# Loads of two tiles by one DMA in a strided mean-removal kernel

## The chip, the cores and the metric

One Trainium2 chip, one core of it. The metric is the device time of one execution in microseconds (us), lower is better. The profile's span is about 1.8 us shorter than that of its own run.

## The reference

```python
def reference(x):                       # x: (8, 4096, 2112) float32, 277 MB
    B, S, D = x.shape
    stride = 4
    x_r = x.reshape(B, S // stride, stride, D)
    pooled = x_r.mean(axis=2)
    upsampled = np.repeat(pooled, stride, axis=1)
    return (x - upsampled).astype(np.float32)
```

From each group of four rows its mean is taken off. 276.8 MB have to be read and as many written.

## The kernel before

A tile is 128 groups: 128 partitions x 8448 floats (33,792 bytes a partition, contiguous in HBM). There are 64 tiles and six slots in SBUF. SyncE issues the loads, VectorE (DVE) sums and subtracts in place, ScalarE's queue issues the stores.

```python
    slots = [io_pool.tile([P, W], f32, name=f"slot{b}") for b in range(SLOTS)]   # SLOTS = 6
    ...
    laps, rest = divmod(n, SLOTS)                                                # n = 64
    with tc.tile_critical():
        for k in range(n):
            b, lap = k % SLOTS, k // SLOTS
            load = nc.sync.dma_start(out=slots[b][:], in_=xg[k * P:(k + 1) * P])
            if lap:
                load._wait_ge(store_sems[b], 16 * lap)
            load.then_inc(load_sems[b], 16)
        # VectorE, each tile: three tensor_add into s, then slot = -s/4 + slot;
        # the first add waits for load_sems[b]
        ...
        for k in range(n):
            b = k % SLOTS
            store = nc.scalar.dma_start(out=og[k * P:(k + 1) * P], in_=slots[b][:])
            store._wait_ge(done_sem, k + 1)
            store.then_inc(store_sems[b], 16)
```

Of the kernel before, what the change touches and what calls it, by code (L numbers as in the profile page):

```python
# [1 line left out]

# [4 lines left out]

STRIDE = 4
SLOTS = 6  # L10
PAD = 224


@with_exitstack
def kernel(
    ctx: ExitStack,
    tc: tile.TileContext,
    x: bass.AP,
    out: bass.AP,
):  # L20






    nc = tc.nc
    B, S, D = x.shape
    P = nc.NUM_PARTITIONS
    W = STRIDE * D  # L30
    G = (B * S) // STRIDE
    assert S % STRIDE == 0 and G % P == 0
    n = G // P

    xg = x.rearrange("b (g f) d -> (b g) (f d)", f=STRIDE)
    og = out.rearrange("b (g f) d -> (b g) (f d)", f=STRIDE)
    f32 = mybir.dt.float32

    pad_pool = ctx.enter_context(tc.tile_pool(name="pad", bufs=1))
    io_pool = ctx.enter_context(tc.tile_pool(name="io", bufs=1))  # L40
    sum_pool = ctx.enter_context(tc.tile_pool(name="sum", bufs=1))
    psum_pool = ctx.enter_context(
        tc.tile_pool(name="psum", bufs=1, space=bass.MemoryType.PSUM)
    )
    pad_pool.tile([P, PAD], f32, name="pad")
    slots = [io_pool.tile([P, W], f32, name=f"slot{b}") for b in range(SLOTS)]
    s_sb = sum_pool.tile([P, D], f32, name="s_sb")
    s_ps = psum_pool.tile([P, D], f32, name="s_ps")

    load_sems = [tc.alloc_semaphore(f"load{b}") for b in range(SLOTS)]  # L50
    store_sems = [tc.alloc_semaphore(f"store{b}") for b in range(SLOTS)]
    step_sem = tc.alloc_semaphore("step")
    done_sem = tc.alloc_semaphore("done")

    adds = STRIDE - 1

    def reduce_tile(b, landed):
        rows = slots[b].rearrange("p (f d) -> p f d", f=STRIDE)
        s = s_ps if b % 2 else s_sb
        done = b * adds  # L60
        for f in range(1, STRIDE):
            first = rows[:, 0, :] if f == 1 else s[:]
            add = nc.vector.tensor_add(out=s[:], in0=first, in1=rows[:, f, :])  # L63
            if f == 1:
                add._wait_ge(load_sems[b], landed)
            else:
                add._wait_ge(step_sem, done + f - 1)
            add.then_inc(step_sem)
        sub = nc.vector.scalar_tensor_tensor(  # L69
            out=rows,  # L70
            in0=s[:, None, :].to_broadcast([P, STRIDE, D]),
            scalar=-1.0 / STRIDE,
            in1=rows,
            op0=mybir.AluOpType.mult,
            op1=mybir.AluOpType.add,
        )
        sub._wait_ge(step_sem, done + adds)
        sub.then_inc(done_sem)

    assert SLOTS % 2 == 0  # L80
    laps, rest = divmod(n, SLOTS)
    with tc.tile_critical():  # L82
        for k in range(n):
            b, lap = k % SLOTS, k // SLOTS
            load = nc.sync.dma_start(out=slots[b][:], in_=xg[k * P:(k + 1) * P])
            if lap:
                load._wait_ge(store_sems[b], 16 * lap)
            load.then_inc(load_sems[b], 16)

        with nc.vector.Fori(0, laps) as lap:  # L90
            landed = nc.vector.to_reg(16 * lap + 16)
            for b in range(SLOTS):
                reduce_tile(b, landed)
            nc.vector.wait_ge(step_sem, SLOTS * adds).then_inc(step_sem, -SLOTS * adds)
        for b in range(rest):
            reduce_tile(b, 16 * (laps + 1))

        for k in range(n):
            b = k % SLOTS
# [5 lines that stand above are left out]
    for k in range(n - SLOTS, n):  # L105
        total = nc.gpsimd.to_reg(16 * (k // SLOTS + 1))
        tc.keep_in_program_order(nc.gpsimd.wait_ge(store_sems[k % SLOTS], total))


# [1 line left out]
_INS = ['x']  # L111
_OUTS = [((8, 4096, 2112), 'float32')]


# [23 lines left out]
```

## Time and profile before

| | before |
|---|---|
| time, median of 6 runs | 1284.84 us (1284.71 to 1285.01) |
| profile's span | 1283.3 us |
| VectorE busy | 1026.5 us, 80% |
| the two DMA queues' packets | 100.1% of 16 engines' span |
| bandwidth, windows in the middle | 433 GB/s (435 in two of the 120 us windows) |
| a tile's period | 19.97 us; VectorE needs 16.1 of it |

How to read it: two queues, one of loads and one of stores, are served by the same 16 DMA engines (their packets fill 50.1% and 50.0% of the engines' span). If the engines always have a packet from one queue or the other, the time is the bytes over 433 GB/s and a few us at the ends: the windows quoted in the prediction show 433 with loads alone (4 to 29 us), with stores alone (1270 to 1280) and with both. VectorE's 20% of idle time and the wait before each tile (3.8 us) are a consequence. The number that decides about the change is not on the page: it is how long a load or store waits in its queue behind others, which is called the queues' spare below. The prediction works it out from the page's times from issue to landing.

### The profile page before, as it was taken

What the parts mean: (1) busy time and instruction counts of PE and PEld (TensorE: products, weight loads), DVE (VectorE), ACT (ScalarE), POOL (GpSimd) and SP (SyncE); (2) the same over time, 40 slices, a digit from 0 to 9 for tenths busy, and PEclk for the clock granted to TensorE, in tenths of its full rate; (3) what the DMA queues carried; (4) which work ended last, traced back from release to release, by engine and by line L of the source; (5) the groups of instructions that cost most, each with busy time, mean ns of one, the idle gap of its engine ahead of it and who ended that gap; (6) DMA issues with size and microseconds to landing.
All of it is one profiled execution on the core that took longest, in us unless ns stands there. A gap on an engine that the chain in (4) does not pass through costs nothing.

```text
span 1283.3 us, 483 instructions
## 1 busy us (share of the span) xinstructions
DVE 1026.5 (80%) x256; POOL 0.2 (0%) x4
## 2 busy tenths in 40 slices
DVE  5998788787887877878778787787877878878785
POOL 0000000000000000000000000000000000000000
DMA  9999999999999999999999999999999999999999
GB/s 404 420 436 429 434 437 434 427 437 436 427 436 437 434 427 437 436 427 436 437 433 428 437 436 426 437 437 433 428 437 434 428 437 437 432 429 437 434 427 404
DMA packets 18432, 553.66 MB, mean 431 GB/s; under 512 B 2048, under 2 KB 2048, under 8 KB 2048
## 3 DMA queue, kind: packets, MB, share of 16 engines
q1 hardware_dynamic: 9216, 276.83, 50.1%
q10 hardware_dynamic: 9216, 276.83, 50.0%
HBM read 276.82 MB, written 276.82 MB: 431 GB/s over the span
## 4 chain that ended last, share of the span: by engine, by line
DVE 73%; another core or an unknown queue 24%; DMA 1%; issue 1%; DVEq 0%; SPq 0%
DVE slot L69 38%; DVE s_ps L63 18%; DVE s_sb L63 18%; DMA slot<-in_x_dram 1%; DVEq L90 0%; SPq L133 0%; SPq L82 0%
## 5 line engine op out<-in xcount | busy, mean ns | idle before, releaser
L69 DVE SCALAR_TENSOR_TENSOR slot<-s_sb,slot 128x8448 f32<-128x8448 f32 x32 | 286.7, 8958 | 1.1
L69 DVE SCALAR_TENSOR_TENSOR slot<-s_ps,slot 128x8448 f32<-128x8448 f32 x32 | 286.6, 8957 | 1.1
L63 DVE TENSOR_TENSOR s_sb<-slot 128x2112 f32<-128x2112 f32 x32 | 75.5, 2358 | 123.7 <-DMA slot<-in_x_dram 123.7
L63 DVE TENSOR_TENSOR s_ps<-slot 128x2112 f32<-128x2112 f32 x32 | 75.7, 2367 | 112.1 <-DMA slot<-in_x_dram 112.1
L63 DVE TENSOR_TENSOR s_ps<-s_ps,slot 128x2112 f32<-128x2112 f32 x64 | 151.4, 2366 | 2.2
L63 DVE TENSOR_TENSOR s_sb<-s_sb,slot 128x2112 f32<-128x2112 f32 x64 | 150.9, 2358 | 2.2
L122 POOL MEMSET const-bfloat16-1.0<- 128x1 bf16 x1 | 0.1, 102 | 0.0
L122 POOL MEMSET const-uint8-127<- 128x1 uint8 x1 | 0.1, 102 | 0.0
L122 POOL MEMSET const-float32-0.0<- 128x1 f32 x1 | 0.1, 99 | 0.2 <-issue 0.2
L122 POOL MEMSET const-float32-1.0<- 128x1 f32 x1 | 0.1, 99 | 0.0
## 6 DMA issues: line engine op xcount, KB each, us to landing
slot<-in_x_dram SPq DMA_DIRECT2D x64, 4224.0 KB, 60.1
out_dram<-slot ACTq DMA_DIRECT2D x64, 4224.0 KB, 43.5
```

Of the source, the lines that this page charges most:

```text
L63: add = nc.vector.tensor_add(out=s[:], in0=first, in1=rows[:, f, :])
L69: sub = nc.vector.scalar_tensor_tensor(out=rows, in0=s[:, None, :].to_broadcast([P, STRIDE, D]), scalar=-1.0 / STRIDE, in1=rows, op0=mybir ...
L122: nc = _bacc.Bacc("TRN2", target_bir_lowering=False, num_devices=1)
```

## The change

Intent: fewer, larger load DMAs. In laps 1 to 9 of the ring one DMA fills two neighbouring slots, with two runs of 33,792 bytes a partition, after both slots' stores have landed. One semaphore stands for both tiles: VectorE waits on it for the first one, and the wait left for the second has long been met. The first six tiles and the last four stay single.

```diff
-    slots = [io_pool.tile([P, W], f32, name=f"slot{b}") for b in range(SLOTS)]
+    ring = io_pool.tile([P, SLOTS * W], f32, name="ring")
+    slots = [ring[:, b * W:(b + 1) * W] for b in range(SLOTS)]
...
-        for k in range(n):
+        k = 0
+        while k < n:
             b, lap = k % SLOTS, k // SLOTS
-            load = nc.sync.dma_start(out=slots[b][:], in_=xg[k * P:(k + 1) * P])
+            size = 2 if 0 < lap < laps else 1
+            if size == 2:
+                nc.sync.wait_ge(store_sems[b], 16 * lap)
+            load = nc.sync.dma_start(
+                out=ring[:, b * W:(b + size) * W].rearrange("p (j w) -> p j w", j=size),
+                in_=xg[k * P:(k + size) * P].rearrange("(j p) w -> p j w", j=size),
+            )
             if lap:
-                load._wait_ge(store_sems[b], 16 * lap)
+                load._wait_ge(store_sems[b + size - 1], 16 * lap)
             load.then_inc(load_sems[b], 16)
+            k += size
...
-                reduce_tile(b, landed)
+                reduce_tile(b, 16 if b % 2 else landed)
...
-            reduce_tile(b, 16 * (laps + 1))
+            reduce_tile(b, 32 if b % 2 else 16 * (laps + 1))
```

## The prediction

> **What bounds the kernel now.** I read the page's busy shares and slices first, then its DMA part and groups, then windows at the start, middle and end, then the timeline of the last tiles.

> The page:

> ```profile
> DVE 1026.5 (80%) x256; POOL 0.2 (0%) x4
> ...
> DMA  9999999999999999999999999999999999999999
> ...
> DMA packets 18432, 553.66 MB, mean 431 GB/s; under 512 B 2048, under 2 KB 2048, under 8 KB 2048
> ...
> q1 hardware_dynamic: 9216, 276.83, 50.1%
> q10 hardware_dynamic: 9216, 276.83, 50.0%
> ...
> slot<-in_x_dram SPq DMA_DIRECT2D x64, 4224.0 KB, 60.1
> out_dram<-slot ACTq DMA_DIRECT2D x64, 4224.0 KB, 43.5
> ```

> VectorE (DVE) is 80% busy, the 16 DMA engines 90% or more in every slice, and the two queues' packets fill 100.1% of 16 engines' span. Apart from 2048 small packets (128 DMAs x 16, the completions), every packet is one 33,792-byte row. The last two lines give each DMA's time from issue to landing; I use them as loop times below.

> The windows (start:end, length, DVE busy, POOL busy, clock, DMA share, GB/s):

> ```profile
> 0.00:4.00 4.00, 0.00 (x0) 0.20 (x4) 1.00 0.66 220
> 4.00:13.00 9.00, 0.00 (x0) 0.00 (x0) 1.00 1.03 443
> 13.00:29.00 16.00, 15.57 (x4) 0.00 (x0) 1.00 0.99 427
> 29.00:35.00 6.00, 5.93 (x4) 0.00 (x0) 1.00 1.03 372
> 35.00:51.00 16.00, 15.90 (x5) 0.00 (x0) 1.00 0.98 425
> ...
> 360.00:480.00 120.00, 96.48 (x25) 0.00 (x0) 1.00 1.00 433
> ...
> 1270.00:1275.00 5.00, 0.00 (x0) 0.00 (x0) 1.00 1.00 433
> 1275.00:1280.00 5.00, 0.00 (x0) 0.00 (x0) 1.00 1.00 433
> 1280.00:1283.30 3.30, 0.00 (x0) 0.00 (x0) 1.00 0.36 154
> ```

> Until 29 us there are only loads: (9 x 443 + 16 x 427) / 25 = 433 GB/s. From 1270 there are only stores: 433. In the middle both: 433. So one queue alone is as fast as two together, and only an interval in which **both** queues are empty costs time. The account of the span: 553.65 MB / 433 = 1278 us, 2.0 us before the first byte (220 GB/s x 4 us is 2.0 us' worth of 433), 2.1 us after the last one, about 1.1 us lost at 29 to 51 us as the first stores start; sum 1283.3, as the page says. The measured time is 1.5 us above that span.

> The timeline of the last tiles (start, length, idle before in brackets):

> ```profile
> 1192.79 2.36 DVE L63 TENSOR_TENSOR s_sb<-slot 128x2112 f32<-128x2112 f32 x1 [3.81 <-DMA slot<-in_x_dram]
> ...
> 1252.69 2.37 DVE L63 TENSOR_TENSOR s_ps<-slot 128x2112 f32<-128x2112 f32 x1 [3.84 <-DMA slot<-in_x_dram]
> 1255.09 4.77 DVE L63 TENSOR_TENSOR s_ps<-s_ps,slot 128x2112 f32<-128x2112 f32 x2
> 1259.89 8.96 DVE L69 SCALAR_TENSOR_TENSOR slot<-s_ps,slot 128x8448 f32<-128x8448 f32 x1
> ```

> Three tiles take 59.90 us, 19.97 each; VectorE needs 16.1 of them and waits 3.8 for a load. VectorE is not the bound. (The chain of waits names VectorE for 73% of the span because it follows semaphores; the wait of 3.8 us before each tile says that the load set the pace.)

> [...]

> **The change part by part.**

> Removed: 27 of 64 load DMAs, with 27 x 16 = 432 completion packets, and no byte of data. [...] SyncE's issue time (0.33 us a DMA) is not on the path.

> Added: a wait in SyncE for the first slot's store. That store ends before the second one's, in the same queue, so it costs nothing beyond the wait for the second.

> Moved: a pair is issued when both its stores have landed, and its first tile can't start before both have landed. The latencies from the trace: a load alone lands 12.4 us after issue and moves for 10.0, so 2.4 of latency; a store alone 13.5, so 3.5. The six slots make a loop, whose length is six tiles, 119.8 us. Before: load 20.0 + 2.4, VectorE 16.1, store 20.0 + 3.5, sum 62.0; the other 57.8 us are waiting in the queues: 60.1 - 22.4 = 37.7 behind other loads, 43.5 - 23.5 = 20.0 behind other stores (sum 57.7, which checks). After, for the second tile of a pair: load 39.9 + 2.4, VectorE 32.1, store 20.0 + 3.5, sum 97.9; 21.9 us of waiting remain. Of these 3.9 are the second store behind the first (20.0 less the 16.1 between their issues). So **18.0 us of spare remain, where there were 57.8**. Still positive: the load queue should never be empty until the last load.

> Where the spare lies follows from the passage from singles to pairs. Before, tile 6 started at 114.7. After, it needs its partner too: about 134.7. VectorE ends tile 5 at 110.9, so it idles 24 us instead of 4, and issues store 6 at 150.7. Stores move one per 20 us from 30.5 on, so store 5 leaves the queue at about 150.5: the store queue is empty for about 1 us (issue to first byte, as at the start: 0.95 to 2.0). Load (8,9), allowed by store 3 at about 113, is in its queue by then and takes the bandwidth. Loss: none. From here stores have next to no spare and loads nearly all 18 us.

> The tail, counted from the landing of pair (58,59) as zero: loads 60 to 63 land at 20, 40, 60, 80, all allowed long before. VectorE runs back to back and ends 58 to 63 at 16, 32, 48, 64, 80.3, 96.4. Stores at half speed: 58 from 17 to 37, 59 to 57, 60 to 77, 61 until the loads end at 78.6 and then alone to 88, 62 to 98; store 63, issued at 96.4, can move from 97.4, in time, to 108. So from the last landing to the end about 30 us, as before (1283.3 - 1252.7 = 30.6), with half a us of spare. A slip here costs what it is, say **0 to 2 us lost**.

> Sum: [...]**1284.5 us**.

> **The rivals.**

> One: three pairs starve the load queue, because SyncE waits for a whole pair. It would cost each pair what the loop exceeds 119.8 by, over three. Speaks for it: the spare falls by two thirds. Against: 18 us stay, five store latencies. If all the spare were mis-sized by 25 us, 7 us of loop or 2.3 a pair would be lost, 62 us, 5% slower, if stores too had run dry; I hold that unlikely.

> Two: VectorE's later start becomes the bound. It has 7.8 us of idle per pair instead of twice 3.9; 32.1 < 39.9. It would matter only in the tail, and the four single tiles are there for that. Pairs to the end would have cost some 10 us; as it is, 0 to 2.

> Three: the addresses. [...] Were this slower in HBM by 2%, for loads alone, 1% of the time, 13 us. Against: the bound is the same 433 for loads, stores and the mix[...]. For it: nothing in this profile.

> Four: fewer, longer DMAs move faster, to 437, the best slices of the page. At most 0.9%, 11 us. Against: windows a lap long all show 433 and the engines have no gap to fill.

> **Range and chances.** The first-order effect is zero, the known terms within 2 us, repeats spread by 0.3 us. [...] The high end, 1289, allows 4 us of slip at the passage and the tail. Over 2% faster (1259.1) needs 553.65 MB in 25.7 us less than 1278, 442 GB/s[...]: 0.01. Over 2% slower (1310.5) needs rival one or three at full size: 0.05. Within: 0.94.

> **What would show it.** Right: 37 loads, 27 of them of twice the size; 8784 packets in the load queue, 1616 small ones; 433 GB/s in every lap; store landing down from 43.5 to 23 to 28 us, a pair's landing about 60 us; VectorE waiting about 7.8 us every second tile, with a total near the old 236 us; one wait of about 24 us at tile 6. Wrong: windows with a DMA share under 0.98 and VectorE waiting over 10 us per pair (rival one), a share of 1.00 at under 430 GB/s (rival three), or over 435 (rival four); or a last store issued well after the store before it has landed (tail).

The forecast's sum came to 1284.5 us: the 1284.84 of before, plus 0 to 2 us lost at the tail, less a gain for the 432 completion packets removed. The range was 1281.5 to 1289 us. In rival three, the order in which an engine takes the rows of a pair and what followed for HBM were assumptions, not shown. Two measured figures: in the trace before, stores land in the order of their issue, some 20 us apart in the middle (the step from the first slot's store to the second's), and of the windows of 120 us two show 435 GB/s and the others 433 (rival four).

## The result

| | before | changed |
|---|---|---|
| time, median of 6 runs each | 1284.84 us | 1285.5 us |
| range | 1284.71 to 1285.01 | 1284.83 to 1286.66 |
| span of the profiled run | 1283.3 us | 1283.4 us |

The ratio of the changed kernel to the one before is 1.0006, 95% interval 0.9993 to 1.0019: no difference that the runs can tell from none. (A ratio is the mean time of one kernel's fast runs over that of the other's of the same rounds, so not quite the ratio of the medians.)

The page of the changed kernel:

```profile
DVE 1023.6 (80%) x256; POOL 0.2 (0%) x4
...
DMA packets 18000, 553.65 MB, mean 431 GB/s; under 512 B 1616, under 2 KB 1616, under 8 KB 1616
...
q1 hardware_dynamic: 8784, 276.83, 50.0%
q10 hardware_dynamic: 9216, 276.83, 50.0%
...
out_dram<-ring ACTq DMA_DIRECT2D x64, 4224.0 KB, 39.9
ring<-in_x_dram SPq DMA_DIRECT2D x27, 8448.0 KB, 42.4
ring<-in_x_dram SPq DMA_DIRECT2D x10, 4224.0 KB, 42.6
```

432 completion packets are gone, as counted, and the queues fill the engines as before. The last three lines are not what was predicted: a pair lands 42.4 us after its issue and not 60, and stores take 39.9 us and not 23 to 28.

Windows of the changed kernel (start:end, length, DVE busy, POOL busy, clock, DMA share, GB/s):

```profile
111.00:131.00 20.00, 0.00 (x0) 0.00 (x0) 1.00 1.00 433
...
360.00:480.00 120.00, 96.21 (x25) 0.00 (x0) 1.00 1.00 434
...
1000.00:1120.00 120.00, 95.99 (x24) 0.00 (x0) 1.00 1.00 433
...
1275.00:1280.00 5.00, 0.00 (x0) 0.00 (x0) 1.00 1.00 433
```

In the first of them VectorE does nothing at all for 20 us, waiting for the first pair, and the engines move 433 GB/s all the same. Its waits in the changed kernel:

```profile
DVE s_sb L66 <- DMA ring<-in_x_dram: 229.3, 28, 23.6
DVE s_ps L66 <- DMA ring<-in_x_dram: 1.0, 1, 1.0
```

Columns: total us, times, the longest. The second tile of a pair never waits (the one time is tile 5, still single); the first one waits for both. The total, some 230 us, is that of before (123.7 + 112.1 = 236), regrouped.

### Where the spare went

The trace's view of a tensor gives the time from issue to landing of the DMAs in a window. Three pair loads of the changed kernel, early, in between and late:

```profile
L92 SPq DMA_DIRECT2D ring<-in_x_dram x1: 379/379/379, 115.1 to 115.1; - x1
...
DMA to landing us min/median/max: 57.9/57.9/57.9
...
L92 SPq DMA_DIRECT2D ring<-in_x_dram x1: 368/368/368, 238.8 to 238.8; - x1
...
DMA to landing us min/median/max: 50.6/50.6/50.6
...
L92 SPq DMA_DIRECT2D ring<-in_x_dram x1: 368/368/368, 642.4 to 642.4; - x1
...
DMA to landing us min/median/max: 42.4/42.4/42.4
```

The same, pair by pair, worked out from the trace's issues and landings of the changed kernel:

```
pair    issued   landed   took   since the pair before
 6,7     74.44   134.32   59.88
 8,9    115.11   173.00   57.89   38.68
10,11   156.35   211.92   55.57   38.92
12,13   197.59   250.60   53.01   38.68
14,15   238.76   289.32   50.56   38.72
16,17   279.94   327.99   48.05   38.68
18,19   321.10   366.68   45.58   38.69
20,21   362.27   405.36   43.08   38.68
22,23   402.85   445.27   42.42   39.92
24,25   442.78   485.19   42.42   39.92
 ... all later pairs: 42.4 to 42.8
```

A pair needs 39.9 us of transfer and 2.4 of latency, 42.3 us, by itself while stores share the engines. So the first pair had 17.6 us of spare, where the prediction had 18, and from pair (22,23) on loads have none. Over the same time the second store of a pair rises from 31.0 us (store 7) to 45.1: the spare moved from the load queue to the store queue, about 2.5 us a pair, and stopped when the loads had none left. The loop is as long as before; only the place of its slack differs.

Two theories for the drift:

And two theories for the time: **only both queues empty** costs anything, which gives figures for shorter rings; or **depth and grouping** themselves matter (or don't, whatever the depth).

### The profile page after: what moved, and what is told of

It is laid out like the page before. It is cut to its first block, busy times and chain, and to the rows that moved or that the text cites. A ratio compares the mean times of both kernels' runs of the same rounds, so it can differ in the third digit from the quotient of the medians.

```text
span 1283.4 us, 483 instructions
## 1 busy us (share of the span) xinstructions
DVE 1023.6 (80%) x256; POOL 0.2 (0%) x4
## 2 busy tenths in 40 slices
DMA  9999999999999999999999999999999999999999
DMA packets 18000, 553.65 MB, mean 431 GB/s; under 512 B 1616, under 2 KB 1616, under 8 KB 1616
## 3 DMA queue, kind: packets, MB, share of 16 engines
q1 hardware_dynamic: 8784, 276.83, 50.0%
q10 hardware_dynamic: 9216, 276.83, 50.0%
## 4 chain that ended last, share of the span: by engine, by line
DMA 55%; DVE 39%; another core or an unknown queue 4%; issue 1%; DVEq 0%; SPq 0%
DMA ring<-in_x_dram 28%; DMA out_dram<-ring 27%; DVE ring L72 21%; DVE s_sb L66 9%; DVE s_ps L66 9%; DVEq L101 0%; SPq L146 0%; SPq L85 0%
## 5 line engine op out<-in xcount | busy, mean ns | idle before, releaser
L72 DVE SCALAR_TENSOR_TENSOR ring<-s_sb,ring 128x8448 f32<-128x8448 f32 x32 | 286.7, 8958 | 1.1
L72 DVE SCALAR_TENSOR_TENSOR ring<-s_ps,ring 128x8448 f32<-128x8448 f32 x32 | 286.6, 8957 | 1.1
L66 DVE TENSOR_TENSOR s_sb<-ring 128x2112 f32<-128x2112 f32 x32 | 75.4, 2357 | 229.3 <-DMA ring<-in_x_dram 229.3
L66 DVE TENSOR_TENSOR s_ps<-s_ps,ring 128x2112 f32<-128x2112 f32 x64 | 151.4, 2366 | 2.2
L66 DVE TENSOR_TENSOR s_sb<-s_sb,ring 128x2112 f32<-128x2112 f32 x64 | 150.9, 2358 | 2.2
L66 DVE TENSOR_TENSOR s_ps<-ring 128x2112 f32<-128x2112 f32 x32 | 75.5, 2359 | 1.0 <-DMA ring<-in_x_dram 1.0
## 6 DMA issues: line engine op xcount, KB each, us to landing
out_dram<-ring ACTq DMA_DIRECT2D x64, 4224.0 KB, 39.9
ring<-in_x_dram SPq DMA_DIRECT2D x27, 8448.0 KB, 42.4
ring<-in_x_dram SPq DMA_DIRECT2D x10, 4224.0 KB, 42.6
```

Of the source, the lines that this page charges most:

```text
L66: add = nc.vector.tensor_add(out=s[:], in0=first, in1=rows[:, f, :])
L72: sub = nc.vector.scalar_tensor_tensor(out=rows, in0=s[:, None, :].to_broadcast([P, STRIDE, D]), scalar=-1.0 / STRIDE, in1=rows, op0=mybir ...
```

## The experiments

All gave correct results. A single core's run is called slow here if it lies over 1.5% above the fastest of the same kernel; for kernels that vary by themselves that label means no more than this.

### 1. The changed kernel again

No edit. 

> The changed kernel once more, beside before. Its first trace showed the load queue running out of spare: a pair's issue to landing falls from 59.9 us by about 2.5 us a pair and stays at 42.4 from pair 9 on, while stores take 39.9 and 45.1. Theory (turns): an engine takes its two queues in turn packet by packet, and a completion packet of 9 ns takes a turn like a row of 1.25 us; a pair of tiles is 17 load turns (16 rows, 1 completion) but 18 store turns (16 rows, 2 completions), so loads gain one row, 1.25 us, a pair. Then the drift repeats exactly. If it was an accident of that run, the medians differ. Time: 1285.5 within 1 us; spread over 1 us, against 0.3 for before, if the missing load spare is what makes it vary.

Measured: 1285.17 us (four runs, 1284.88, 1285.08, 1285.26, 1286.67) against 1285.01 (1284.82 to 1285.58, 11 runs): ratio 1.0003, interval 0.999 to 1.0016. The drift repeats in this run, half a step ahead: 58.6, 56.3, 53.8, 51.2, 48.7, 46.2, 43.7, then 42.5. So it is no accident of one run. The changed kernel has a run over 1286 in both sets and before has none, but the cause of that is not settled here.

### 2. The gate alone

Two single loads, issued together when both stores have landed.

```diff
+            for j in range(size):
+                load = nc.sync.dma_start(out=slots[b + j][:], in_=xg[(k + j) * P:(k + j + 1) * P])
+                if lap and j == 0:
+                    load._wait_ge(store_sems[b + size - 1], 16 * lap)
+                load.then_inc(load_sems[b + j], 16)
```

> The change's gate alone: two single loads issued together when both stores have landed, each with its own semaphore. Same landing times as before (a tile lands every 19.97 us), no wait of 24 us at tile 6, stores at 43.5, first load of a couple at about 40, second at 60. 1284.8 to 1285.2.

Measured: 1285.61 us in one run (before 1284.73, median of 7 of the same rounds). Its issues:

```profile
ring<-in_x_dram SPq DMA_DIRECT2D x64, 4224.0 KB, 59.3
out_dram<-ring ACTq DMA_DIRECT2D x64, 4224.0 KB, 43.9
```

(The median of the loads mixes 39.7 for the first of a couple and 59.3 for the second.) Neither moves: with 18 turns on either side, nothing drifts in this kernel, and waiting for both stores shows no cost of its own, as far as one run can tell (it is 0.4 us above the slowest of the seven of before).

### 3. Four slots, single tiles

`SLOTS = 4` in the kernel before. 

> The kernel before with four slots instead of six: the loop is four tiles, 79.9 us, and needs 62.0 (load 22.4, VectorE 16.1, store 23.5), so 17.9 us of spare stay, as many as the changed kernel has. If only an empty loop spare costs time: 1284.8 within 2 us. If depth itself matters: slower.

Measured: 1289.68 us (1288.58 to 1289.86), ratio 1.0038, interval 1.0021 to 1.0055. Loads land in 28.6 us and stores in 35.0; less 22.4 and 23.5 that is 17.7 us of spare, as worked out (how far the 23.5 holds is said under "Why"). In the middle the rate is 433 to 434 in every window. But the time is 4.9 us longer, where at most 2 were expected. Windows of the four-slot kernel:

```profile
51.00:131.00 80.00, 69.07 (x18) 0.00 (x0) 1.00 1.01 428
...
1265.00:1270.00 5.00, 4.97 (x2) 0.00 (x0) 1.00 1.02 439
1270.00:1275.00 5.00, 4.50 (x1) 0.00 (x0) 1.00 0.44 189
```

At 1270 to 1275 the share is 0.44: 2.8 us without a packet. The store queue had 11.5 us of spare instead of 20, so store 62 had landed (1273.4) before VectorE had finished tile 63 and its store was issued (1274.5). Another us or so went at 51 to 131 us (428, where before has 435). The ratio lies under the 2% that counts as a difference here, but its interval is clear of 1. Spare was worth nothing in the middle here, but the share of it that lies in the **store** queue is what covers VectorE's last tile.

### 4. Four slots, pairs

The changed kernel with `SLOTS = 4` and `laps, rest = n // SLOTS - 1, SLOTS`. 

> The change on four slots: first four and last four tiles singly, 28 pairs between. The loop of two pairs needs 97.9 us at half speed and has 79.9. With the transfers' speeds shared as they overlap, the period per pair comes out as 40.0 of transfers plus the 3.5 us in which both queues are empty[...]: 43.5 instead of 39.9. 28 x 3.6 = 100 us, so about 1385 us (1360 to 1400), DMA share 0.92 in the middle. If grouping costs nothing whatever the depth: 1285.

Measured: 1380.92 us (1379.99 to 1383.17), ratio 1.0745, interval 1.0727 to 1.0763. A window of it:

```profile
600.00:710.00 110.00, 75.81 (x21) 0.00 (x0) 1.00 0.96 404
```

The share falls under 1, which it did over no whole lap of the kernels so far. From the landing at 356.4 to the one at 702.1 lie eight pairs, 43.2 us each; 43.5 had been worked out. The size is right, but not all of what it was made of: a share of 0.92 was expected and 0.96 came. The 3.5 us with both queues empty was the estimate. By the packet records of these eight pairs an engine has no packet for only 1.9 us a pair. Another 1.5 us is load rows that take 1.3 to 3.0 us instead of 1.25: nearly all are the first row of a load after the gap, or the last two before the next store's first row, so where a queue starts up. Grouping cost 7% here, where the ring's spare is negative.

### 5. Six slots, loads of three

```diff
-            size = 2 if 0 < lap < laps else 1
+            size = 3 if 0 < lap < laps else 1
```

(and waits for three stores.) 

> Six slots, loads of three tiles (18 of them, first six and last four singly): two groups in the ring. Loop need at half speed 59.9 + 2.4 + 48.2 + 23.5 = 134 against 119.8. The same working as for four slots in pairs: 60.0 of transfers plus 3.5 us of both queues empty, 63.5 a triple instead of 59.9: 18 x 3.6 = 65 us, about 1350 (1330 to 1365). If larger DMAs help: under 1285.

Measured: 1346.34 us (1346.01 to 1347.24), ratio 1.0481, interval 1.0463 to 1.0498. A window of it:

```profile
800.00:920.00 120.00, 89.37 (x22) 0.00 (x0) 1.00 0.97 414
```

Triples land 63.1 us apart (398.0 to 903.0, eight of them; 63.5 worked out, 59.9 when the engines are full). Here too 1.7 us of the 3.2 lost are without a packet and 1.5 are slow load rows. The first size that no longer fits the six slots is three.

### 6. Pairs to the end

`size = 2 if lap else 1`, so that tiles 60 to 63 too come in pairs. 

> The changed kernel with the last four tiles in pairs too. The prediction put this at some 10 us. From the trace of the changed kernel: the last pair lands where its last single did, at 1244; VectorE then needs 32.1 us, so store 63 is issued at 1276 instead of 1260.6 and lands 13.5 later, at 1289.7, against 1282.5: about 7 us slower, 1292 to 1293. If the end is set by bytes alone: 1285.

Measured: 1292.03 us (1289.94 to 1292.43) against 1285.08: ratio 1.0055, interval 1.0038 to 1.0072, 7 us. The timeline of the kernel with pairs to the end:

```profile
1243.54 2.36 DVE L66 TENSOR_TENSOR s_sb<-ring 128x2112 f32<-128x2112 f32 x1 [7.71 <-DMA ring<-in_x_dram]
...
1266.79 8.96 DVE L72 SCALAR_TENSOR_TENSOR ring<-s_ps,ring 128x8448 f32<-128x8448 f32 x1
```

The last pair lands at 1243.5 and VectorE has two tiles to do after it: it ends at 1275.8, and the last store lands at 1287.1. Store 62 had landed at 1272.2, so there is a stretch in which both queues are empty, as expected. The profile is of the fastest of the four runs (1289.94 us). The last store took 11.3 us in it and not the 13.5 expected; those came from the kernel before, whose last store was issued (1268.9) before store 62 had landed (1272.4). The four single tiles at the end earn 5 to 7 us.

### 7. Pairs from the start

The first six tiles in pairs too. 

> The changed kernel with the first six tiles in pairs too. VectorE starts 10 us later (23.3 instead of 13.3), but the load queue has 60 us of work, so the DMA engines have no gap: if only both queues empty costs time, 1285 within 1.5 us. If a later start of VectorE counts: up to 10 us slower.

Measured: 1286.36 us (1286.08 to 1287.56) against 1285.08: ratio 1.0009, interval 0.9992 to 1.0026. VectorE starts at 23.3 instead of 13.3, and the time is not 10 us longer. All four runs lie above all seven of before, by 1.3 us in the median; that is within the interval, and what it comes from was not looked into. So a VectorE that starts 10 us late cost 1.3 us in the median here, with the load queue full.

### 8. The load of a pair in two halves of 64 partitions

To give the load queue 18 turns a pair, at the same gate and with both tiles still landing together:

```diff
+            H = P // size
+            for h in range(size):
+                load = nc.sync.dma_start(out=dst[h * H:(h + 1) * H], in_=src[h * H:(h + 1) * H])
```

> Each pair load issued as two DMAs of 64 partitions, both runs each: same gate, same landing of both tiles together, but two completions a pair, so 18 load turns against 18 store turns. Turns: no drift; second half's issue to landing stays at 57 to 60 us, the first half's at about 40, stores stay at 25 to 31 us, VectorE waits 7.8 us a pair from the first pair on. Rival (loads gain because the store queue runs empty at each burst of VectorE, or because the DMA is long): the same drift as the changed kernel, second half down to 42.4 us, stores up to 40 and 45. Time 1284.8 to 1285.5 in either case; nearer 1284.8 with a spread of 0.3 us if spare on the load side is what keeps before steady.

Measured: 1627.87 us (1462.89 to 1740.94), profiled in the run of 1740.94, the slowest; the figures of its rows are those of that run alone. The two fast runs give a ratio of 1.1443. A window of the halves:

```profile
600.00:720.00 120.00, 64.37 (x17) 0.00 (x0) 1.00 1.01 306
```

A share of 1.01 at 306 GB/s: the queues are full, and rows are slow. A load row takes 2.08 us (median) where it took 1.25. The run tells nothing of the drift, as its premise, that a split leaves the rows' speed alone, was false.

### 9. Stores of the kernel before in two halves

```diff
+            for h in range(2):
+                lo, hi = h * P // 2, (h + 1) * P // 2
+                store = nc.scalar.dma_start(out=og[k * P + lo:k * P + hi], in_=slots[b][lo:hi, :])
```

> The kernel before, with each store issued as two DMAs of 64 partitions: 10 store turns a tile (8 rows, 2 completions) against 9 load turns. Turns: loads gain about 1 us a tile, so that a load's issue to landing falls from 60.1 by about 2 us a tile and stays at about 22.4 from some 19 tiles on, and the second half of a store rises from 43.5 to about 81. Rival (drift belongs to pair loads): loads stay at 60.1, stores at 43.5. Time 1284.8 in either case, within 2 us, as one of the queues always has work.

Measured: 1391.62 us (1347.61 to 1425.42). Loads land in 34.2 us (median; 60.1 before) and halves of stores in 56.1, so the spare does go over to the stores, in single-tile loads too. But rows are slow here as well (means of 1.32 and 1.39 us), so this agrees with turns and does not prove them.

### 10. Loads of the kernel before in two halves

The mirror of the last one. 

> The mirror: each load of the kernel before as two DMAs of 64 partitions, 10 load turns against 9 store turns. Turns: stores gain; a store's issue to landing falls from 43.5 to about 24 (an empty store queue), the second half of a load rises from 60.1 to about 80. Rival: 43.5 and 60.1 stay. Time 1284.8, within 2 us.

Measured: 1526.26 us, one run. Stores land in 29.0 us (43.5 before), halves of loads in 87.5 (60.1): the direction turns round, as expected, with the same reservation (load rows of 1.62 us on the mean).

### 11. A tiny load after each pair

One more packet and one more completion for each engine and pair on the mean, in the load queue (its packets rise from 8784 to 9648, by 27 x 32): 19 turns against 18. The pair load stays one long DMA.

```diff
+            if size == 2:
+                c = k // 2
+                tiny = nc.sync.dma_start(out=pad[0:16, c:c + 1], in_=xg[0:16, c:c + 1])
+                tiny.then_inc(tiny_sem, 16)
```

> The changed kernel, and after each pair load a load of 16 partitions by 4 bytes into unused space, on the same queue: one more packet and one more completion on each engine, so 19 load turns a pair against 18 store turns, at some 20 ns of transfer. Turns: the drift turns round, stores gain until their queue is empty, and all spare stays with the loads: a pair's issue to landing stays at 57 to 60 us to the end, stores at 24 to 29 us, VectorE waits 7.8 us from the first pair on. Rivals (long DMA, bursts of VectorE): the drift of the changed kernel, 42.4 and 40 to 45 us. Time: 1285.0 to 1285.5 with little spread if missing load spare costs the changed kernel its few tenths; but with stores early the tail has no spare, as the prediction had it, so 0 to 3 us may be lost there: 1285 to 1288.

Measured: 1314.9 us (1313.28 to 1324.54), ratio 1.0252, interval 1.0219 to 1.0285. The issues of the kernel with tiny loads:

```profile
out_dram<-ring ACTq DMA_DIRECT2D x64, 4224.0 KB, 27.2
ring<-in_x_dram SPq DMA_DIRECT2D x27, 8448.0 KB, 62.4
```

The drift of the changed kernel is gone: pairs take 58.5 us at first, up to 66.3 on the way and 61.3 at the end, stores 24 to 31. A long DMA does not by itself draw the spare away from the loads. The time, however, rose by 30 us where 0 to 3 were expected. From 131 us on the windows give 422 to 425 GB/s at a share of 1.00, and the mean row takes 1.286 us in the load queue and 1.265 in the store queue, against 1.254 and 1.251: slower rows again, not empty queues. With 8 rows of each kind an engine and tile that is 8 x (0.032 + 0.014) x 64 = 24 us of the 28 by which the span grew. Why 27 loads of 64 bytes slow the rows is open.

### 12. Halves of even and odd partitions

Experiment 8 with `dst[h::size]` and `src[h::size]`. The reason to try it: if the slow rows of experiment 8 (2.08 us) come from which partitions a half holds, another choice of halves may bring 1.25 us back; if any split is slow, it will not. 

> The pair loads again as two DMAs, but of the even and the odd partitions instead of the lower and upper 64. [...]the rows come back to 1.25 us and the time to about 1285; then with 18 turns on either side the drift is gone (turns): second half near 60 us, stores 24 to 31. If any split of a DMA's partitions is slow: about 1600 again.

Measured: 1324.01, 1338.72, 1285.61 and 1337.72 us. The median row is back at 1.251 us in both queues. One run is as fast as the kernel before, the others lose 3 to 4%; in the profiled one (1324.01, of the slower kind) the rate holds 433 GB/s until about 310 us and decays after. Its first 310 us are a clean test of the drift. The pair loads of even and odd halves at 114 and at 274 us:

```profile
L95 SPq DMA_DIRECT2D ring<-in_x_dram x2: 601/668/736, 114.3 to 114.9; - x2
...
DMA to landing us min/median/max: 39.7/49.4/59.0
...
L95 SPq DMA_DIRECT2D ring<-in_x_dram x2: 602/607/612, 274.0 to 274.6; - x2
...
DMA to landing us min/median/max: 39.7/49.4/59.1
```

The second half takes 59.0 us and four pairs later still 59.1. In the changed kernel these same pairs fell from 57.9 to about 48. VectorE waits 7.7 us before each pair, so it works in the same bursts. Apart from the split itself, only the count of completions differs.

What follows: bursts are excluded (12 has them, and no drift), length is excluded (11 has it, and no downward drift), and the drift stops where the turns are equal, 18 to 18 (2, 12), and has the size of one row a pair where they are 17 to 18.

No view prints the order in which an engine serves its queues, but the packet records of the kept traces hold it. They name queue, start and length of each packet; the engine follows from the times, as a row starts within some ns of the end of the one before it, and the rows fall into 16 chains of 1024. In the kernel before, from 111 to 360 us, rows of the two queues alternate in all 3190 cases, and so they do in all 3188 of the gate alone. In the changed kernel, over the same six pairs, two load rows follow each other 191 times and two store rows 95 times: twice and once for each pair and engine. A completion of the store queue lies between the two load rows in 179 of the 191 cases, and the load's completion between the two store rows in 89 of the 95. So a completion does take the turn of a row.

In the halves of even and odd partitions there are 3 exceptions in 2548 cases up to 310 us. The half-partition slowness depends on which partitions a half holds: load rows took 2.08 us (median) in halves of 64 neighbours and 1.251 in even and odd halves. Why was not shown. Three of four runs with even and odd halves still being slow (1324 to 1339 us) shows that it isn't all of it.

## Why the prediction was right or wrong

- **The bound and the time: right.** 1284.5 was predicted, 1285.5 measured, within the range (1281.5 to 1289). While the rows keep their speed, only an interval with both queues empty cost time: the changed kernel has a share of 1.00 through the 20 us in which VectorE stands still, and where the spare was made negative (4, 5) the same loop arithmetic gave 43.5 and 63.5 us where 43.2 and 63.1 were measured (with about half of the loss in slow rows and not in empty queues).
- **The spare of 18.0 us: right within some 2 us.** In the late steady state the load takes 42.4 us, VectorE 32.1 for a pair, the second store 45.1. The store's 45.1 less 23.5 is 21.6, less the 3.9 behind the first store 17.7; the load has 0.1. This is less of a check than it looks, as the three parts always fill the loop of 119.8 us. The load's 42.4 is confirmed, the store's 23.5 is not: its latency of 3.5 us came from a last store of 13.5 us that was issued before store 62 had landed. Last stores that were truly alone took 11.3 us (3 to 6), a latency of 1.4; the first store of the kernel before, beside loads and in an empty queue, took 25.1, a latency of 5.
- **Where the spare lies: wrong.** The step "From here stores have next to no spare and loads nearly all 18 us" held for the first pair (59.9 us to landing) and was then undone within eight pairs. The prediction took two full queues to share the engines equally in bytes. They share equally in turns, and the change takes away one load completion in two while the stores keep theirs; the packet records show each completion in the place of a row. The trace says this also for the prediction's signs: pairs landing in 42.4 us and not 60, stores in 39.9 and not 23 to 28.
- **The gain from fewer completions: not shown.** Its term in the forecast rested on a figure that no trace shows. The packet records give a completion 9 ns, so the 27 fewer of each engine are 0.24 us, below what the runs can tell.
- **The passage at tile 6: right in its outcome.** A wait of 23.6 us, and nothing lost. The store queue was not empty for 1 us, though: store 6 was issued at 150.5, and store 5 landed only at 156.3.
- **The tail: no slip, but partly by luck.** Because the loads had run ahead, the last one landed at 1243.9, 8.7 us before that of the kernel before. VectorE was done at 1260.5, and the last store then took 21.9 us, 10.5 more than the 11.3 of one truly alone: that many us of spare and not 0.5. The drift that the prediction had missed earned them. In experiment 11, where the drift is gone, the last store took 12.6 us, 1.2 of spare, which is near the half; but the rows are slow there. This also puts the cost of pairs to the end at 5 to 7 us, where the prediction had some 10.
- **The rivals.** Starvation (one) came true in a harmless form: from pair (22,23) on each load finds its queue just empty, but stores fill the engines. It cost time only where the spare of both queues was gone (7.5% and 4.8% in 4 and 5). Addresses (three) and a faster rate for large DMAs (four): the rate is 433 to 434 in the windows of the middle, as before.

The 0.7 us between the medians lie within the interval of no difference; no cause is claimed for them, nor for the wider scatter of the changed kernel. No experiment points to a faster version: 1278 of the 1283 us are the bytes at 433 GB/s.

## What to carry to other kernels

For a kernel bound by DMA, add up one loop of the buffer ring (load, compute, store, latencies) at the shared speed and compare it with the slots times the period: while the rest was positive, grouping loads did not change the time here, and once it was negative each group lost 3.2 to 3.4 us, about half of it with both queues empty and half in slow rows as they started again. Count the DMAs of both queues too: where each completion takes the turn of a row, the queue with fewer completions draws the spare away from the other (2.5 us a pair here, at 17 turns against 18), and that decides what covers the tail. Keep the last tiles single, since compute after the last landing was covered only by what still waits in the store queue (5 to 7 us here). Do not split a DMA by partition ranges without measuring it (loads in halves of 64 partitions took 1463 to 1741 us here, against 1285).
